# A one-dimensional average pool over 512 MB: larger input tiles, pairwise sums in place of a reduction, and another order of the last stores

## The chip, the cores and the metric

The kernel runs on one core of one Trainium2 chip. The metric is the time of one execution on the device in microseconds (us); the median of a few runs is quoted. The engines that matter here are VectorE (DVE in the profile), ScalarE (ACT), SyncE (SP), which only issues transfers here, and the 16 DMA engines of the core, which move data between HBM and SBUF, the on-chip memory of 128 partitions.

## The reference

The input `x` has 64 x 256 rows of 8192 float32. Each row is cut into windows of 4 elements that do not overlap, and the output is the mean of each window, 2048 values per row.

```
for i in range(out_len):                 # out_len = (8192 - 4) // 4 + 1 = 2048
    start = i * stride                   # stride = kernel_size = 4
    output[:, :, i] = np.mean(x[:, :, start : start + kernel_size], axis=2)
```

So 536.87 MB are read, 134.22 MB are written, and there are three additions and one scaling for each output.

## The kernel before

The shapes send the call to `_packed_fast_path` (the other path of the file, with its loops over `NT`, is not used). It takes F = 4 neighbouring rows for each partition, so that one group is 512 rows: 128 partitions with 32,768 consecutive input elements (128 KB) and 8192 consecutive output elements (32 KB) each. There are 32 groups, the loop over `t`.

In a group the loop over `f` handles the four rows one after the other. Each step takes a tile `xt` of 8192 elements (32 KB) per partition from the pool `xin`, which has three buffers. One load fills it from the SP queue (L245), one `tensor_reduce` on VectorE sums each window of four into a quarter of the output tile `ot` (L246), and `nc.scalar.mul` scales that quarter by 1/4 in place on ScalarE (L252). When all four quarters are there, one store of 32 KB per partition goes out from the ACT queue (L253). `ot` has two buffers.

A load can be issued as soon as its buffer is free, that is when the reduction three steps earlier has read it. The loads are issued in program order by SP, which waits for that reduction. The framework places all waits from these buffers; no order is written out by hand, except at the end.

The last group (from L258) is cut finer. Its row 0 is one load; rows 1 and 2 are each loaded in three pieces of about 2730 elements (L263, with reductions at L266 and scalings at L272). Row 3 is loaded in a ladder of six pieces that shrink from 2268 to 608 elements (L284, reductions at L293). Five of these pieces are scaled on ScalarE (L309) and stored from the ACT queue (L310); the last is scaled on VectorE into a small tile `fin` (L300) and stored from SP (L307). Rows 0 to 2 of this group, 24 KB per partition, are held back: they are stored from SP in four pieces right after the last load was issued (L292), so that the DMA engines have work while the last pieces are reduced.

```
if last:
    qw = hold // _N_PARK
    for qi in range(_N_PARK):
        ...
        nc.sync.dma_start(out=ov[:, qa:qb], in_=ot[:, qa:qb])
```

Of the kernel before, what the change touches and what calls it, by code (L numbers as in the profile page):

```python
# [7 lines left out]
_N_PARK = 4  # L8
_FINAL_COLS_TGT = 608
_LADDER_RATIO = 1.39  # L10
_NCHUNK_PRE = 3
_PACK_STORES = True
_PACK_F_MAX = 4


def _tail_ladder(total: int, k: int, final: int, ratio: float = _LADDER_RATIO,
                 max_chunks: int = 12) -> list:
    if total < 4 * final:
        return [total]
    rev = []  # L20
    s = 0
    w = float(final)
    while len(rev) < max_chunks - 1:
        wi = max(k, (int(round(w)) // k) * k)
        if s + wi > total - k:
            break
        rev.append(wi)
        s += wi
        w *= ratio
    sizes = [total - s] + rev[::-1]  # L30
    assert sum(sizes) == total and all(x > 0 and x % k == 0 for x in sizes)
    return sizes


def _even_chunks(total: int, k: int, n: int) -> list:
    n = max(1, min(n, total // k))
    q = (total // n) // k * k
    sizes = [q] * n
    sizes[-1] += total - q * n
    assert sum(sizes) == total and all(s > 0 and s % k == 0 for s in sizes)  # L40
    return sizes


@with_exitstack
def kernel(
    ctx: ExitStack,
    tc: tile.TileContext,
    x: bass.AP,
    kernel_size: bass.AP,
    stride: bass.AP,  # L50
    out: bass.AP,
):
    nc = tc.nc

    K = int(kernel_size)
    S = int(stride)
    assert K == S, "only stride == kernel_size supported"

    B, C, L = x.shape
    OL = (L - K) // S + 1  # L60
    assert OL * K <= L

    P = nc.NUM_PARTITIONS

    xf = x.flatten_outer_dims()
    of = out.flatten_outer_dims()
    rows = B * C

    inv_k = 1.0 / float(K)
    dt = x.dtype  # L70
    IL = OL * K

    if _PACK_STORES and IL == L:
        F = 0
        for cand in range(_PACK_F_MAX, 1, -1):
            if rows % (P * cand) == 0 and (rows // (P * cand)) >= 2:
                F = cand
                break
        if F >= 2 and L >= 64 * K and OL % 8 == 0 and OL * F * 4 <= 32768:
            _packed_fast_path(nc, tc, xf, of, rows, L, OL, K, F, inv_k, dt, P)  # L80
            return

    RPP = 1
    R = P * RPP
    NT = rows // R
    IL2 = RPP * L
    OL2 = RPP * OL
    fast = (
        IL == L
        and rows % R == 0  # L90
        and NT >= 6
        and IL2 >= 64 * K
        and OL % 2 == 0
    )

    if not fast:
        with (
            tc.tile_pool(name="xin", bufs=4) as pin,
            tc.tile_pool(name="res", bufs=4) as pout,
        ):  # L100
            r0 = 0
            while r0 < rows:
                rn = min(P, rows - r0)
                xt = pin.tile([P, IL], dt)
                ot = pout.tile([P, OL], dt)
                nc.sync.dma_start(out=xt[:rn], in_=xf[r0 : r0 + rn, :IL])
                nc.vector.tensor_reduce(
                    out=ot[:rn],
                    in_=xt[:rn].rearrange("p (m k) -> p m k", k=K),
                    axis=mybir.AxisListType.X,  # L110
                    op=mybir.AluOpType.add,
                )
                nc.scalar.mul(ot[:rn], ot[:rn], inv_k)
                nc.scalar.dma_start(out=of[r0 : r0 + rn], in_=ot[:rn])
                r0 += P
        return

    def xview(t):
        return xf[t * R : (t + 1) * R]

    def oview(t):
        return of[t * R : (t + 1) * R]

    ladder = _tail_ladder(IL2, K, _FINAL_COLS_TGT)
    chunks_pre = _even_chunks(IL2, K, _NCHUNK_PRE)
    fin_w = ladder[-1] // K

    with (
        tc.tile_pool(name="xin", bufs=4) as pin,
        tc.tile_pool(name="res", bufs=4) as pout,  # L130
        tc.tile_pool(name="rsv", bufs=1) as prsv,
        tc.tile_pool(name="fin", bufs=1) as pfin,
    ):
        rsv = prsv.tile([P, OL2], dt)
        fin = pfin.tile([P, fin_w], dt)

        for t in range(NT):
            xv = xview(t)
            ov = oview(t)
            xt = pin.tile([P, IL2], dt)  # L140
            ot = rsv if t == 0 else pout.tile([P, OL2], dt)

            if t == 0:
                nc.sync.dma_start(out=xt[:, :IL2], in_=xv[:, :IL2])
                nc.vector.tensor_reduce(
                    out=ot[:, :OL2],
                    in_=xt[:, :IL2].rearrange("p (m k) -> p m k", k=K),
                    axis=mybir.AxisListType.X,
                    op=mybir.AluOpType.add,
                )  # L150
                nc.scalar.mul(ot[:, :OL2], ot[:, :OL2], inv_k)
            elif t < NT - 3:
                nc.sync.dma_start(out=xt[:, :IL2], in_=xv[:, :IL2])
                nc.vector.tensor_reduce(
                    out=ot[:, :OL2],
                    in_=xt[:, :IL2].rearrange("p (m k) -> p m k", k=K),
                    axis=mybir.AxisListType.X,
                    op=mybir.AluOpType.add,
                )
                nc.scalar.mul(ot[:, :OL2], ot[:, :OL2], inv_k)  # L160
                nc.scalar.dma_start(out=ov[:, :OL2], in_=ot[:, :OL2])
            elif t < NT - 1:
                c0 = 0
                for cw in chunks_pre:
                    c1 = c0 + cw
                    o0, o1 = c0 // K, c1 // K
                    nc.sync.dma_start(out=xt[:, c0:c1], in_=xv[:, c0:c1])
                    nc.vector.tensor_reduce(
                        out=ot[:, o0:o1],
                        in_=xt[:, c0:c1].rearrange("p (m k) -> p m k", k=K),  # L170
                        axis=mybir.AxisListType.X,
                        op=mybir.AluOpType.add,
                    )
                    nc.scalar.mul(ot[:, o0:o1], ot[:, o0:o1], inv_k)
                    nc.scalar.dma_start(out=ov[:, o0:o1], in_=ot[:, o0:o1])
                    c0 = c1
            else:
                nchunk = len(ladder)
                c0 = 0
                for i, cw in enumerate(ladder):  # L180
                    c1 = c0 + cw
                    o0, o1 = c0 // K, c1 // K
                    last = i == nchunk - 1
                    nc.sync.dma_start(out=xt[:, c0:c1], in_=xv[:, c0:c1])
                    if last:
                        q0 = 0
                        qw = (OL2 - q0) // _N_PARK
                        for qi in range(_N_PARK):
                            qa = q0 + qi * qw
                            qb = q0 + (qi + 1) * qw if qi != _N_PARK - 1 else OL2  # L190
                            nc.sync.dma_start(
                                out=oview(0)[:, qa:qb], in_=rsv[:, qa:qb]
                            )
                    nc.vector.tensor_reduce(
                        out=ot[:, o0:o1],
                        in_=xt[:, c0:c1].rearrange("p (m k) -> p m k", k=K),
                        axis=mybir.AxisListType.X,
                        op=mybir.AluOpType.add,
                    )
                    if last:  # L200
                        nc.vector.tensor_scalar(
                            out=fin[:, :fin_w],
                            in0=ot[:, o0:o1],
                            scalar1=inv_k,
                            scalar2=None,
                            op0=mybir.AluOpType.mult,
                        )
                        nc.sync.dma_start(out=ov[:, o0:o1], in_=fin[:, :fin_w])
                    else:
                        nc.scalar.mul(ot[:, o0:o1], ot[:, o0:o1], inv_k)  # L210
                        nc.scalar.dma_start(out=ov[:, o0:o1], in_=ot[:, o0:o1])
                    c0 = c1


def _packed_fast_path(nc, tc, xf, of, rows, L, OL, K, F, inv_k, dt, P):
    R = P * F
    NTM = rows // R

# [10 lines left out]
    with (  # L229
# [6 lines left out]
        for t in range(NTM):  # L236
            xv = xe(t)
# [109 lines left out]
```

## Time and profile before

| | |
|---|---|
| median of 3 runs (lowest, highest) | 1561.05 us (1560.87, 1561.38) |
| span of the profiled execution, first to last instruction | 1559.0 us |
| VectorE busy | 1112.8 us (71%) in 138 instructions |
| ScalarE busy | 247.4 us (16%) |
| read from HBM, written to HBM | 536.87 MB, 134.22 MB |
| DMA rate over the span | 430 GB/s |

The profile gives of its execution the span, and no other time; the median of the runs is 2.0 us above that span, and these 2.0 us lie outside the first and the last instruction. The profile also has groups of instructions (line, engine, operation, output and input tile, count, busy time, mean duration, and the idle time before them with what ended it), a timeline in order of time, and windows, which tell for a stretch of time how long each engine was busy and what the DMA engines moved. "DMA share" is the mean busy share of the 16 DMA engines; as overlapping packets are both counted, it can be a little over 1.

### The profile page before, as it was taken

The numbers are of one execution on the slowest core, as the hardware profiler recorded it, in microseconds if no ns is written. First come the engines' busy times: TensorE is split into PE (matmuls) and PEld (weight loads), VectorE is DVE, ScalarE is ACT, GpSimd is POOL, SyncE is SP. The second block draws the span as 40 slices with busy tenths as digits, with TensorE's granted clock in tenths as the row PEclk, the third lists the DMA queues.
The fourth block names the chain that finished last, engine by engine and source line by source line (L and its number), as shares of the span: only waits on it lengthen the run. The fifth ranks groups of instructions, "written<-read, shape, count | busy, mean of one in ns | idle before, by whom it ended". The sixth has DMA issues, their size and how long they took to land.

```text
span 1559.0 us, 724 instructions
## 1 busy us (share of the span) xinstructions
DVE 1112.8 (71%) x138; ACT 247.4 (16%) x137; POOL 0.2 (0%) x4
## 2 busy tenths in 40 slices
DVE  6777667776667866677666776667766677766786
ACT  1111111111111111111111111111111111111111
POOL 0000000000000000000000000000000000000000
DMA  9999999999999999999999999999999999999999
GB/s 416 418 430 436 437 432 430 430 430 432 439 433 430 430 432 430 438 434 431 430 432 430 435 434 433 431 431 430 433 437 433 432 430 431 430 437 434 432 427 384
DMA packets 25637, 671.14 MB, mean 430 GB/s; under 512 B 2848, under 2 KB 3488, under 8 KB 4768
## 3 DMA queue, kind: packets, MB, share of 16 engines
q1 hardware_dynamic: 20448, 540.10, 80.6%
q10 hardware_dynamic: 5184, 131.00, 19.5%
q14 instruction: 5, 0.04, 0.0%
HBM read 536.87 MB, written 134.22 MB: 430 GB/s over the span
## 4 chain that ended last, share of the span: by engine, by line
DMA 75%; DVE 24%; issue 0%; SPq 0%; DVEq 0%
DMA xt<-in_x_dram 75%; DVE ot L246 23%; DVE ot L293 1%; DVE ot L266 0%; SPq L263 0%; DVEq L246 0%; DVE fin L300 0%
## 5 line engine op out<-in xcount | busy, mean ns | idle before, releaser
L246 DVE TENSOR_REDUCE ot<-xt 128x2048 f32<-128x8192 f32 x124 | 1077.1, 8686 | 430.2 <-DMA xt<-in_x_dram 430.2
L252 ACT ACTIVATE ot<-ot 128x2048 f32<-128x2048 f32 x124 | 237.0, 1911 | 1270.2 <-DVE ot L246 1270.2
L266 DVE TENSOR_REDUCE ot<-xt 128x682 f32<-128x2728 f32 (+2 forms) x7 | 26.6, 3809 | 6.9 <-DMA xt<-in_x_dram 6.9
L272 ACT ACTIVATE ot<-ot 128x682 f32<-128x682 f32 (+2 forms) x7 | 6.6, 936 | 25.8 <-DVE ot L266 25.8
L293 DVE TENSOR_REDUCE ot<-xt 128x417 f32<-128x1668 f32 (+5 forms) x6 | 9.0, 1568 | 0.0
L309 ACT ACTIVATE ot<-ot 128x417 f32<-128x417 f32 (+4 forms) x5 | 2.6, 521 | 5.2 <-DVE ot L293 5.2
L252 ACT ACT_TABLE_LOAD x1 | 1.3, 1283 | 0.7 <-PEq L328 0.7
L300 DVE TENSOR_SCALAR fin<-ot 128x152 f32<-128x152 f32 x1 | 0.2, 239 | 0.0
L328 POOL MEMSET const-bfloat16-1.0<- 128x1 bf16 x1 | 0.1, 102 | 0.0
L328 POOL MEMSET const-uint8-127<- 128x1 uint8 x1 | 0.1, 102 | 0.0
L328 POOL MEMSET const-float32-0.0<- 128x1 f32 x1 | 0.1, 99 | 0.2 <-issue 0.2
L328 POOL MEMSET const-float32-1.0<- 128x1 f32 x1 | 0.1, 99 | 0.0
## 6 DMA issues: line engine op xcount, KB each, us to landing
xt<-in_x_dram SPq DMA_DIRECT2D x125, 4096.0 KB, 26.4
out_dram<-ot ACTq DMA_DIRECT2D x31, 4096.0 KB, 23.2
xt<-in_x_dram SPq DMA_DIRECT2D x4, 1364.0 KB, 23.4
out_dram<-ot SPq DMA_DIRECT2D x4, 768.0 KB, 7.7
xt<-in_x_dram SPq DMA_DIRECT2D x2, 1368.0 KB, 29.5
xt<-in_x_dram SPq DMA_DIRECT2D x1, 1134.0 KB, 16.2
xt<-in_x_dram SPq DMA_DIRECT2D x1, 834.0 KB, 22.6
xt<-in_x_dram SPq DMA_DIRECT2D x1, 816.0 KB, 17.8
```

Source lines behind the costliest of these rows:

```text
L246: nc.vector.tensor_reduce(out=ot[:, o0 : o0 + OL], in_=xt[:, :L].rearrange("p (m k) -> p m k", k=K), axis=mybir.AxisListType.X, op=mybir.A ...
L252: nc.scalar.mul(ot[:, o0 : o0 + OL], ot[:, o0 : o0 + OL], inv_k)
L266: nc.vector.tensor_reduce(out=ot[:, o0:o1], in_=xt[:, c0:c1].rearrange("p (m k) -> p m k", k=K), axis=mybir.AxisListType.X, op=mybir.AluOp ...
L272: nc.scalar.mul(ot[:, o0:o1], ot[:, o0:o1], inv_k)
L293: nc.vector.tensor_reduce(out=ot[:, o0:o1], in_=xt[:, c0:c1].rearrange("p (m k) -> p m k", k=K), axis=mybir.AxisListType.X, op=mybir.AluOp ...
L300: nc.vector.tensor_scalar(out=fin[:, :fin_w], in0=ot[:, o0:o1], scalar1=inv_k, scalar2=None, op0=mybir.AluOpType.mult,)
L309: nc.scalar.mul(ot[:, o0:o1], ot[:, o0:o1], inv_k)
L328: nc = _bacc.Bacc("TRN2", target_bir_lowering=False, num_devices=1)
```

## The change

The whole kernel is written anew. The grouping of rows, 128 KB of input and 32 KB of output per partition and group, is the same, and so are the addresses and sizes of the loads and stores outside the last groups. What differs:

- A tile `xt` has 16,384 elements (64 KB) per partition, and the pool has two of them in place of three of 32 KB. Two loads of 32 KB per partition fill one tile (L71). A group has two tiles, 64 in all (the loop over `n`).
- The sum of four is taken in two steps by `tensor_tensor` on VectorE, over the whole tile: neighbours are added in place into the tile's first half (L52: 8192 outputs), then neighbours of these sums go to `ot` (L57: 4096 outputs). ScalarE scales 4096 elements at once (L58).
- A store from the ACT queue (L84) follows each group up to group 29. Those of groups 30 and 31 are issued from SP after the last load.
- The last tile is loaded in two pieces of 11,264 and 5,120 elements. Behind them SP issues the store of all of group 30 (L74) and of the first half of group 31 (L75), and then one store for each of the two pieces (L81) when it is summed and scaled. The three-piece rows, the ladder, `fin`, and the five small stores from ACT are gone.

```diff
-        tc.tile_pool(name="xin", bufs=3) as pin,
-        tc.tile_pool(name="res", bufs=2) as pout,
-        tc.tile_pool(name="fin", bufs=1) as pfin,
...
-                    xt = pin.tile([P, L], dt)
-                    o0 = f * OL
-                    nc.sync.dma_start(out=xt[:, :L], in_=xv[:, f * L : (f + 1) * L])
-                    nc.vector.tensor_reduce(
-                        out=ot[:, o0 : o0 + OL],
-                        in_=xt[:, :L].rearrange("p (m k) -> p m k", k=K),
-                        axis=mybir.AxisListType.X,
-                        op=mybir.AluOpType.add,
-                    )
-                    nc.scalar.mul(ot[:, o0 : o0 + OL], ot[:, o0 : o0 + OL], inv_k)
-                nc.scalar.dma_start(out=ov[:, : F * OL], in_=ot[:, : F * OL])
...
+LOAD = 16384
+PER_STORE = 2
+HALVES = (8192, 8192)
+LAST = (11264, 5120)
...
+    run = LOAD * PER_STORE
+    total = x.shape[0] * x.shape[1] * x.shape[2]
+    groups = total // (P * run)
...
+    pin = ctx.enter_context(tc.tile_pool(name="xin", bufs=2))
+    pout = ctx.enter_context(tc.tile_pool(name="res", bufs=2))
 
+    def pool(xt, at, width, ot, to):
+        half = width // 2
+        four = xt[:, at : at + width].rearrange("p (m k) -> p m k", k=2)
+        nc.vector.tensor_tensor(
+            out=xt[:, at : at + half], in0=four[:, :, 0], in1=four[:, :, 1], op=ADD
+        )
+        two = xt[:, at : at + half].rearrange("p (m k) -> p m k", k=2)
+        o = ot[:, to : to + width // K]
+        nc.vector.tensor_tensor(out=o, in0=two[:, :, 0], in1=two[:, :, 1], op=ADD)
+        nc.scalar.mul(o, o, inv_k)
...
+    for n in range(groups * PER_STORE):
+        g, j = divmod(n, PER_STORE)
+        last = n == groups * PER_STORE - 1
+        if j == 0:
+            tiles[g] = pout.tile([P, run // K], dt, name="ot")
+        ot = tiles[g]
+        xt = pin.tile([P, LOAD], dt)
+        at = 0
+        for w in LAST if last else HALVES:
+            lo = j * LOAD + at
+            nc.sync.dma_start(out=xt[:, at : at + w], in_=xg[g][:, lo : lo + w])
+            at += w
+        if last:
+            nc.sync.dma_start(out=og[g - 1], in_=tiles[g - 1][:, :])
+            nc.sync.dma_start(out=og[g][:, : j * LOAD // K], in_=ot[:, : j * LOAD // K])
+        at = 0
+        for w in LAST if last else (LOAD,):
+            to = (j * LOAD + at) // K
+            pool(xt, at, w, ot, to)
+            if last:
+                nc.sync.dma_start(out=og[g][:, to : to + w // K], in_=ot[:, to : to + w // K])
+            at += w
+        if j == PER_STORE - 1 and g < groups - 2:
+            nc.scalar.dma_start(out=og[g], in_=ot[:, :])
```

More of the change, by code (lines that the diff above doesn't have):

```diff
@@ L6 @@
 from concourse._compat import with_exitstack
[L8 to L41, printed above, removed]
+ADD = mybir.AluOpType.add
+LOAD = 16384
+PER_STORE = 2
+HALVES = (8192, 8192)
+LAST = (11264, 5120)
 @with_exitstack
@@ L55 @@
     K = int(kernel_size)
[L56 to L61, printed above, removed]
+    assert K == 4 and int(stride) == 4 and x.shape[-1] % 4 == 0
     P = nc.NUM_PARTITIONS
[L65 to L69, printed above, removed]
     dt = x.dtype
[L71 to L93, printed above, removed]
-    )
[L96 to L106, printed above, removed]
-                nc.vector.tensor_reduce(
-                    out=ot[:rn],
-                    in_=xt[:rn].rearrange("p (m k) -> p m k", k=K),
-                    axis=mybir.AxisListType.X,
-                    op=mybir.AluOpType.add,
-                )
[L113 to L131, printed above, removed]
-        tc.tile_pool(name="fin", bufs=1) as pfin,
[L133 to L212, printed above, removed]
@@ L215, in _packed_fast_path @@
-def _packed_fast_path(nc, tc, xf, of, rows, L, OL, K, F, inv_k, dt, P):
-    R = P * F
-    NTM = rows // R
-    ladder = _tail_ladder(L, K, _FINAL_COLS_TGT)
-    chunks_pre = _even_chunks(L, K, _NCHUNK_PRE)
-    fin_w = ladder[-1] // K
-    def xe(t):
-        return xf[t * R : (t + 1) * R].rearrange("(p f) m -> p (f m)", f=F)
-    def oe(t):
-        return of[t * R : (t + 1) * R].rearrange("(p f) m -> p (f m)", f=F)
-    with (
-        tc.tile_pool(name="xin", bufs=3) as pin,
-        tc.tile_pool(name="res", bufs=2) as pout,
-        tc.tile_pool(name="fin", bufs=1) as pfin,
-    ):
-        fin = pfin.tile([P, fin_w], dt)
-        for t in range(NTM):
-            xv = xe(t)
-            ov = oe(t)
-            ot = pout.tile([P, F * OL], dt)
-            if t < NTM - 1:
-                for f in range(F):
-                    xt = pin.tile([P, L], dt)
-                    o0 = f * OL
-                    nc.sync.dma_start(out=xt[:, :L], in_=xv[:, f * L : (f + 1) * L])
-                    nc.vector.tensor_reduce(
-                        out=ot[:, o0 : o0 + OL],
-                        in_=xt[:, :L].rearrange("p (m k) -> p m k", k=K),
-                        axis=mybir.AxisListType.X,
-                        op=mybir.AluOpType.add,
-                    )
-                    nc.scalar.mul(ot[:, o0 : o0 + OL], ot[:, o0 : o0 + OL], inv_k)
-                nc.scalar.dma_start(out=ov[:, : F * OL], in_=ot[:, : F * OL])
-                continue
-            for f in range(F - 1):
-                xt = pin.tile([P, L], dt)
-                widths = [L] if f < F - 3 else chunks_pre
-                c0 = 0
-                for cw in widths:
-                    c1 = c0 + cw
-                    o0, o1 = f * OL + c0 // K, f * OL + c1 // K
-                    nc.sync.dma_start(
-                        out=xt[:, c0:c1], in_=xv[:, f * L + c0 : f * L + c1]
-                    )
-                    nc.vector.tensor_reduce(
-                        out=ot[:, o0:o1],
-                        in_=xt[:, c0:c1].rearrange("p (m k) -> p m k", k=K),
-                        axis=mybir.AxisListType.X,
-                        op=mybir.AluOpType.add,
-                    )
-                    nc.scalar.mul(ot[:, o0:o1], ot[:, o0:o1], inv_k)
-                    c0 = c1
-            fq = F - 1
-            xt = pin.tile([P, L], dt)
-            hold = fq * OL
-            nchunk = len(ladder)
-            c0 = 0
-            for i, cw in enumerate(ladder):
-                c1 = c0 + cw
-                o0, o1 = fq * OL + c0 // K, fq * OL + c1 // K
-                last = i == nchunk - 1
-                nc.sync.dma_start(
-                    out=xt[:, c0:c1], in_=xv[:, fq * L + c0 : fq * L + c1]
-                )
-                if last:
-                    qw = hold // _N_PARK
-                    for qi in range(_N_PARK):
-                        qa = qi * qw
-                        qb = (qi + 1) * qw if qi != _N_PARK - 1 else hold
-                        nc.sync.dma_start(out=ov[:, qa:qb], in_=ot[:, qa:qb])
-                nc.vector.tensor_reduce(
-                    out=ot[:, o0:o1],
-                    in_=xt[:, c0:c1].rearrange("p (m k) -> p m k", k=K),
-                    axis=mybir.AxisListType.X,
-                    op=mybir.AluOpType.add,
-                )
-                if last:
-                    nc.vector.tensor_scalar(
-                        out=fin[:, :fin_w],
-                        in0=ot[:, o0:o1],
-                        scalar1=inv_k,
-                        scalar2=None,
-                        op0=mybir.AluOpType.mult,
-                    )
-                    nc.sync.dma_start(out=ov[:, o0:o1], in_=fin[:, :fin_w])
-                else:
-                    nc.scalar.mul(ot[:, o0:o1], ot[:, o0:o1], inv_k)
-                    nc.scalar.dma_start(out=ov[:, o0:o1], in_=ot[:, o0:o1])
-                c0 = c1
@@ new lines @@
+    inv_k = 1.0 / K
+    run = LOAD * PER_STORE
+    total = x.shape[0] * x.shape[1] * x.shape[2]
+    groups = total // (P * run)
+    assert groups * P * run == total and groups >= 2
+    xg = x.flatten_outer_dims().rearrange("r l -> (r l)").rearrange("(g p w) -> g p w", p=P, w=run)
+    og = out.flatten_outer_dims().rearrange("r l -> (r l)").rearrange(
+        "(g p w) -> g p w", p=P, w=run // K
+    )
+    pin = ctx.enter_context(tc.tile_pool(name="xin", bufs=2))
+    pout = ctx.enter_context(tc.tile_pool(name="res", bufs=2))
@@ new lines @@
+    tiles = {}
+    for n in range(groups * PER_STORE):
[22 more added lines that the diff above has]
+            nc.scalar.dma_start(out=og[g], in_=ot[:, :])
```

## The prediction

> **What bounds the kernel now.** I read the page first: busy times, the row of DMA rates, the two queues.
>
> ```profile
> span 1559.0 us, 724 instructions
> DVE 1112.8 (71%) x138; ACT 247.4 (16%) x137; POOL 0.2 (0%) x4
> ...
> DMA  9999999999999999999999999999999999999999
> ...
> q1 hardware_dynamic: 20448, 540.10, 80.6%
> q10 hardware_dynamic: 5184, 131.00, 19.5%
> ```
>
> The packets of the two queues (SP's q1, ACT's q10) fill 100% of the time of 16 DMA engines. The kernel is bound by transfers; VectorE waits 430 us for loads. Any time to gain is where the engines are not busy, or busy and moving little. The windows show where that is (columns: length; busy time of DVE, ACT, POOL; clock; DMA share; GB/s).
>
> ```profile
> 10.00:50.00 40.00, 34.21 (x4) 5.73 (x3) 0.00 (x0) 1.00 1.00 433
> 50.00:54.00 4.00, 2.97 (x2) 1.91 (x1) 0.00 (x0) 1.00 0.91 393
> 54.00:58.00 4.00, 4.00 (x1) 0.00 (x0) 0.00 (x0) 1.00 1.09 369
> 58.00:60.00 2.00, 2.00 (x1) 0.00 (x0) 0.00 (x0) 1.00 0.72 311
> ...
> 1500.00:1520.00 20.00, 18.86 (x3) 3.82 (x3) 0.00 (x0) 1.00 1.00 428
> 1520.00:1540.00 20.00, 14.26 (x5) 3.86 (x5) 0.00 (x0) 1.00 1.00 423
> 1540.00:1550.00 10.00, 9.91 (x8) 3.38 (x6) 0.00 (x0) 1.00 1.02 413
> ...
> 1552.00:1554.00 2.00, 0.00 (x0) 0.00 (x0) 0.00 (x0) 1.00 1.08 405
> 1554.00:1556.00 2.00, 0.00 (x0) 0.00 (x0) 0.00 (x0) 1.00 0.88 344
> 1556.00:1557.00 1.00, 0.00 (x0) 0.00 (x0) 0.00 (x0) 1.00 0.18 71
> ```
>
> From 60 to 1500 us every window of 200 us gives 432 or 433 GB/s: nothing is left there. Near 50 to 60 us, where ACT issues its first store (52.51 us), the rate dips; against 433 GB/s this loses 0.37 + 0.59 + 0.56 = 1.5 us. Later stores show no dip. From 1500 to 1554 the engines are fully busy but move less, in the stretch of small pieces; from 1554 some engines are done before others.
>
> Third, groups by form and the timeline, for durations.
>
> ```profile
> L246 DVE TENSOR_REDUCE ot<-xt 128x2048 f32<-128x8192 f32 x124 | 1077.1, 8686 | 430.2 <-DMA xt<-in_x_dram 430.2
> L252 ACT ACTIVATE ot<-ot 128x2048 f32<-128x2048 f32 x124 | 237.0, 1911 | 1270.2 <-DVE ot L246 1270.2
> L266 DVE TENSOR_REDUCE ot<-xt 128x682 f32<-128x2728 f32 x4 | 12.0, 2993 | 1.5 <-DMA xt<-in_x_dram 1.5
> L272 ACT ACTIVATE ot<-ot 128x682 f32<-128x682 f32 x4 | 3.1, 772 | 9.2 <-DVE ot L266 9.2
> L300 DVE TENSOR_SCALAR fin<-ot 128x152 f32<-128x152 f32 x1 | 0.2, 239 | 0.0
> ```
>
> The first load is issued at 0.73 us and the first reduction starts at 12.74; the next start at 22.43, 32.14 and 41.85. So a load of 4.19 MB takes 9.70 us of the engines (432 GB/s), and issue plus landing add 12.01 - 9.70 = 2.3 us.
>
> **The change, part by part.** *Loads and stores.* The bytes, addresses and 32 KB rows of 126 loads and 30 ACT stores are as before; at 432 GB/s they cost the same. The question is only whether the SP queue ever runs dry.
>
> *Sums.* VectorE goes from 8.69 us per 8192 inputs to two passes per 16,384. No row shows a tensor-tensor addition or an operand with a step of two. The two reduction rows give (8686 - 2993) / (8192 - 2728) = 1.042 ns per element and 151 ns fixed. If a pass costs by its outputs (two operands read side by side), it is 8.69 + 4.42 = 13.1 us per tile. If it costs by the inputs read, one at a time, it is 17.2 + 8.7 = 25.9 us. The low end is the L300 row's (239 - 151) / 152 = 0.58 ns per element: 7.4 us. I take 13.1, since the reduction's row is one element per step and an addition step makes one output. VectorE's sum is 64 x 13.1 = about 840 us (54%). ACT takes 4096 elements at 0.834 ns + 203 ns (its two rows) = 3.6 us, 232 us in all, hidden beside loads.
>
> *Two buffers.* A tile's two loads take 2 x 9.70 = 19.4 us of the engines. When tile n lands, tile n+1 is queued; tile n+2 is issued after the two passes and its data flows 2.3 us later (this counts landing too). The queue is refilled 13.1 + 2.3 = 15.4 us after the landing, 4.0 us before tile n+1 is through. A store in flight only lengthens that cover. So no gap, and both signs of the VectorE price up to 17.1 us per tile cost nothing. Before, the margin was 2 x 9.70 - 8.69 - 2.3 = 8.4 us.
>
> *Added waits.* Pass 1 waits for two loads in place of one; behind it are pass 2, the scaling and SP's next loads, all counted above. Pass 2 waits for pass 1: L300, which reads what L293 just wrote, starts at 1549.71, 0.04 us after L293's last end. Pass 2 of a new group also waits for the store two groups back, issued over 50 us earlier, where stores land within 23.2 us. At the end SP waits at L75 for the scaling of tile 62 and has only L81's stores behind it.
>
> The Trainium skill ("VectorE: DVE Perf Modes", section "The DRAIN you can't avoid") puts a drain of the operation's duration less 266 ns behind every VectorE operation. Taken as coming on top, it would start pass 2 8.4 us later, the tile would take 21.5 us, and by the rival's price below the time would be about 1700 us. The six back-to-back reductions at L293, 9.0 us busy in 9.02 us of the timeline, speak against that reading.
>
> *The tail.* Removed: six loads of 1364 to 1368 KB, six ladder loads, five small ACT stores, L307, four stores of 768 KB. What they cost is the fully busy stretch below 433 GB/s: 20 x 5/433 + 20 x 10/433 + 10 x 20/433 = 1.15 us up to 1550, and 0.08 (416 GB/s) + 0.13 from there to 1554: 1.4 us. Added: two load pieces, the half store, and two stores of 1408 and 640 KB. The first three have rows of 16 KB or more, larger than the cut rows were: taken as 0.1 us. The last two move 2.1 MB in 4.8 us at 2 to 5% loss: 0.15 us. Net -1.1 us; bounds 0 and -1.4.
>
> Does the last sum hide? From the last landing L, the queue still holds group 30 (4.19 MB, 9.7 us) and half of group 31 (4.85 us): busy until L + 14.5. Tile 62 landed at L - 19.4, and its passes end at about L - 5.7; piece one takes 5632 and 2816 outputs, 9.1 us, to L + 3.4; piece two 4.3 us, to L + 7.7; its scaling 1.3 us, and at most the 2.3 us of issue, to L + 11.3. That is 3.2 us before the parked stores are through, and piece one's store lies between (3.3 us). So the queue stays full to the last byte. What remains is the spread of the engines after 1554 and the end after the last landing: (2 - 1.59) + 0.84 + 0.97 + 1.04 = 3.3 us, kept.
>
> The Trainium skill ("DMA: Bandwidth & Descriptors", section "Anatomy of one DMA") gives each transfer about 2.0 us of fixed cost. There are 178 issues before and 162 after; if each cost were exposed, 16 x 2.0 = 32 us would go, to 1529 us. The landings 9.70 us apart while loads are queued say that it is hidden.
>
> **Sum.** Span 1559.0 - 1.1 = 1557.9 us; the 2.0 us outside it are kept: 1559.9 us.
>
> **The rivals.** 0.2% is 3.1 us, about what a measurement of this kernel can tell from no change.
>
> *Slower: VectorE starves the queue.* It decides from 17.1 us per tile on. Beyond that the engines stand idle once per group of two tiles (a store covers the other boundary), 32 us for each us. At the by-input price of 25.9 us, a tile's loads take 21.7 us after issue, 31.4 with a store in between; the pace alternates between 25.9 and 31.4, 28.7 x 64 = 1835 us. For it: no row shows such an addition, with two operands of step two and an output over its own input. Against it: 13.1 would have to be wrong by 30%. 0.12.
>
> *Slower, a little: two buffers do not keep the queue full*, because an engine that lags delays the landing, by more than the 4.0 us of margin. A gap of 0.1 us per tile is 6.4 us: 1566 us. The spread after 1554, some 2 to 3 us, speaks against it. 0.06.
>
> *Faster: more of the losses go.* If the dip at 50 to 60 us (-1.5) does not come back and the engines end 1 us closer together, it is 1557.4 us. For it: stores after the first show no dip; against it: ACT still has a first store. 0.13.
>
> *The forecast*, 0.69, has its own range of 1558.3 to 1561.5: 1559.9 and the tail's bounds, with the spread of the engines 1 us either way.
>
> **Numbers.** Faster by over 0.2% (below 1557.9) is the faster rival, 0.13; same 0.69; slower 0.12 + 0.06 = 0.18. The range goes down to 1556.5 (the tail's full 1.4, the dip's 1.5 and 1.6 of the spread) and up to 1566, the small gap's price; what is left out is mostly the starved queue.
>
> **What would show it.** Right: L52 near 8.7 and L57 near 4.4 us, VectorE near 54%; windows at 432 to 433 GB/s from 60 us to some 10 us before the end, also past 1540; a dip near 57 us. Wrong: windows below 430 in the middle, or passes of 17 us and more together (starved queue); a higher rate in the middle than 433 would break the argument altogether, since I hold that for what the engines can do.

## The result, and the profile after

The changed kernel takes 1569.18 us, the median of 5 runs (1567.99 to 1570.91), against 1561.15 us for the kernel before in the same comparison: a ratio of 1.0052, 95% interval 1.0040 to 1.0064. It is slower by 8.0 us, or 0.5%, where 1559.9 us and no measurable change were predicted; the range ended at 1566.0. Medians in this document are over all runs of a kernel; the ratios are not quotients of these medians and leave out one disturbed run of e8, so that the two can differ a little where the runs scatter (e8, e9, h4, k2).

The page of the changed kernel (its profiled execution took 1570.91 us):

```profile
span 1569.1 us, 619 instructions
DVE 839.8 (54%) x130; ACT 232.9 (15%) x66; POOL 0.2 (0%) x4
...
GB/s 414 414 439 430 429 433 433 429 434 433 431 430 430 433 427 425 430 426 434 423 434 433 430 429 427 424 425 422 433 433 429 428 431 433 427 423 433 427 435 379
...
q1 hardware_dynamic: 19008, 545.27, 81.4%
q10 hardware_dynamic: 4320, 125.83, 18.6%
```

The busy times are those of the prediction, and the two queues still fill 100% of the engines' time: nothing ran dry. But the row of rates, one number for each 39 us, falls below 430 again and again after the first third. The groups by form agree with the priced durations to 0.01 us:

```profile
L52 DVE TENSOR_TENSOR xt<-xt 128x8192 f32<-128x8192 f32 x63 | 547.6, 8693 | 712.1 <-DMA xt<-in_x_dram 712.1
L57 DVE TENSOR_TENSOR ot<-xt 128x4096 f32<-128x4096 f32 x63 | 278.8, 4425 | 3.8
L58 ACT ACTIVATE ot<-ot 128x4096 f32<-128x4096 f32 x63 | 227.8, 3616 | 1316.2 <-DVE ot L57 1316.2
```

The windows of the changed kernel (columns as in the prediction) show where the time is. The same windows of the kernel before give 433 GB/s; the second of them is shown below the others.

```profile
200.00:400.00 200.00, 106.77 (x17) 31.58 (x9) 0.00 (x0) 1.00 1.00 432
600.00:800.00 200.00, 109.31 (x17) 28.93 (x8) 0.00 (x0) 1.00 1.00 429
1000.00:1200.00 200.00, 109.04 (x17) 28.93 (x8) 0.00 (x0) 1.00 1.00 428
```

```profile
600.00:800.00 200.00, 143.87 (x17) 30.58 (x16) 0.00 (x0) 1.00 1.00 433
```

The DMA share is 1.00 in each of the four: after the change the engines are as busy, and move 1% less. 1% of the 1000 us from 500 to 1500 us is 10 us, the size of the loss. It is not in the tail.

To see what is slow I used the trace's record of each DMA packet, put in a row for each engine. A packet of 32 KB (one partition's row of a load or store) takes 1213 ns in both kernels, and the packets of an engine follow each other without gaps (0.3 us of idle time per engine in all). But some packets take longer. Summed over all 32-KB packets above 1230 ns, their time beyond 1213 ns, divided by 16 engines, is **before** 1.6 us up to 75 us (mainly at the first store) and 0.1 us from there on, from 5 packets; **after** 1.8 us and then 11.6 us, from 572 packets. This sum after 75 us is called the stretch below. The gap to a kernel without it, f1 below, is 11.1 us of span (1569.1 against 1558.0).

Some four fifths of this time is in load packets that run 0.5 to 4.5 us after an ACT store was issued, on each engine the one or two just before its first packet of that store. Around one store, the timeline of the changed kernel:

```profile
971.53 8.69 DVE L52 TENSOR_TENSOR xt<-xt 128x8192 f32<-128x8192 f32 x1 [16.75 <-DMA xt<-in_x_dram]
980.26 4.42 DVE L57 TENSOR_TENSOR ot<-xt 128x4096 f32<-128x4096 f32 x1
984.71 0.80 SPq L71 DMA_DIRECT2D xt<-in_x_dram  x2
984.71 3.62 ACT L58 ACTIVATE ot<-ot 128x4096 f32<-128x4096 f32 x1 [26.28 <-DVE ot L57]
988.36 0.34 ACTq L84 DMA_DIRECT2D out_dram<-ot  x1
990.96 8.69 DVE L52 TENSOR_TENSOR xt<-xt 128x8192 f32<-128x8192 f32 x1 [6.28 <-DMA xt<-in_x_dram]
```

and its windows from that store on, and between stores (a window counts each packet whole where it starts, so that short windows are exact only to some per cent):

```profile
988.00:1000.00 12.00, 8.95 (x2) 0.33 (x1) 0.00 (x0) 1.00 1.02 404
1006.00:1030.00 24.00, 9.02 (x2) 1.82 (x1) 0.00 (x0) 1.00 1.00 430
```

The tile that the queue is working on lands just before 990.96, when its pass 1 starts. The two loads behind it were issued at 984.71, the store at 988.36. So the engines cross from one tile's loads to the next one's right around the store's issue, and the 12 us from the store on run at 404 GB/s.

The loss builds up. By "spread" I mean the time between the first and the last of the 16 engines to finish the same load. In the kernel before it is 0.5 us early and 1.3 us at 850 us. In the changed kernel the stores up to 500 us cost 0.05 to 0.3 us each, on some of the engines; the spread grows from 0.4 to 3.4 us by 550 us. Of the 20 stores from 547.76 us on, 12 hit all 16 engines and cost 0.4 to 1.0 us each; the other 8 cost at most 0.3 us.

### The profile page after: what moved, and what is told of

Read it like the earlier page. It is cut to its first block, busy times and chain, and to the rows that moved or that the text cites. A ratio compares the mean times of both kernels' runs of the same rounds, so it can differ in the third digit from the quotient of the medians.

```text
span 1569.1 us, 619 instructions
## 1 busy us (share of the span) xinstructions
DVE 839.8 (54%) x130; ACT 232.9 (15%) x66; POOL 0.2 (0%) x4
## 4 chain that ended last, share of the span: by engine, by line
DMA 71%; DVE 27%; SPq 1%; issue 0%; ACT 0%; DVEq 0%
DMA xt<-in_x_dram 71%; DVE xt L52 18%; DVE ot L57 9%; SPq L71 1%; ACT ot L58 0%; DVEq L52 0%
## 5 line engine op out<-in xcount | busy, mean ns | idle before, releaser
L52 DVE TENSOR_TENSOR xt<-xt 128x8192 f32<-128x8192 f32 (+1 forms) x65 | 556.5, 8561 | 712.1 <-DMA xt<-in_x_dram 712.1
L58 ACT ACTIVATE ot<-ot 128x4096 f32<-128x4096 f32 (+1 forms) x65 | 231.6, 3564 | 1323.5 <-DVE ot L57 1323.5
L57 DVE TENSOR_TENSOR ot<-xt 128x4096 f32<-128x4096 f32 (+1 forms) x65 | 283.4, 4360 | 3.9
## 6 DMA issues: line engine op xcount, KB each, us to landing
out_dram<-ot SPq DMA_DIRECT2D x1, 1408.0 KB, 12.6
out_dram<-ot SPq DMA_DIRECT2D x1, 640.0 KB, 11.1
```

Of the source, the lines that this page charges most:

```text
L52: nc.vector.tensor_tensor(out=xt[:, at : at + half], in0=four[:, :, 0], in1=four[:, :, 1], op=ADD)
L57: nc.vector.tensor_tensor(out=o, in0=two[:, :, 0], in1=two[:, :, 1], op=ADD)
L58: nc.scalar.mul(o, o, inv_k)
```

## The experiments

The kernels are named by the labels e1 to k2. Unless it is said otherwise, diffs are against the changed kernel. Four theories were tested. *Store start*: an ACT store that starts while engines cross into freshly issued loads slows the loads. *Late refill*: with two buffers the next loads are issued only 1 to 6 us before an engine needs them, and that costs time by itself. *Burst*: two loads issued at once disturb the queue. *Sums*: the new VectorE passes disturb the DMA's writes into SBUF.

**e4, the sums alone** (the kernel before, its reduction replaced by the two passes).

```diff
-                    nc.vector.tensor_reduce(... ot[:, o0 : o0 + OL] ...)
+                    nc.vector.tensor_tensor(out=xt[:, : L // 2], in0=four[:, :, 0], in1=four[:, :, 1], ...)
+                    nc.vector.tensor_tensor(out=ot[:, o0 : o0 + OL], in0=two[:, :, 0], in1=two[:, :, 1], ...)
```

> The kernel before with the reduction at L246 replaced by the two pairwise passes, nothing else: three buffers of 32 KB, 6.7 us instead of 8.7 us per tile. Both theories: no change, 1560 to 1562 us; a store is issued 2 us earlier relative to the loads. If the pairwise passes themselves disturbed the transfers (two operands read, written in place): 1566 us or more.

1561.22 us (1560.91 to 1561.68), ratio 1.0001 (0.9993 to 1.0010). The pairwise sums by themselves change nothing in the time.

**e1, four tiles of 32 KB**, so that loads are queued deeper. Everything else, the tail too, is as changed.

```diff
-LOAD, PER_STORE, HALVES, LAST = 16384, 2, (8192, 8192), (11264, 5120)
+LOAD, PER_STORE, HALVES, LAST = 8192, 4, (8192,), (5632, 2560)
-    pin = ctx.enter_context(tc.tile_pool(name="xin", bufs=2))
+    pin = ctx.enter_context(tc.tile_pool(name="xin", bufs=4))
```

> The changed kernel with four buffers of 32 KB in place of two of 64 KB: one load, two passes and one scaling per 8192 elements, same SBUF, same stores, same tail order (last load in pieces of 5632 and 2560 elements). The queue is refilled some 20 us before it would run dry instead of 4. Store issue is about 9 us after a landing, again within 1 us of the next load boundary. Late-refill theory (engines that lead run out of queued loads): the loss goes, 1559 to 1561 us, rate 432 to 433 GB/s throughout. Store-start theory (a store that starts near a load boundary disturbs the engines whatever is queued): most of the loss stays, 1566 to 1570 us.

1560.27 us (1559.87 to 1560.76), ratio 0.9995 (0.9986 to 1.0004); stretch 0.2 us. The loss is gone, against the expectation from the store start. But the run also moves the store: the slowest engine crosses into the next load 0.5 us after the store's issue, where it is 2.1 us in the changed kernel. So it does not tell a deeper queue from a moved store.

**e3, no stores in the middle.** The ACT stores of groups 0 to 29 are left out.

```diff
-        if j == PER_STORE - 1 and g < groups - 2:
-            nc.scalar.dma_start(out=og[g], in_=ot[:, :])
```

> The changed kernel without the 30 stores from ACT (the outputs of groups 0 to 29 are not written). 125.8 MB less, 291 us at 432 GB/s. Every load boundary now has the short margin, not every second one. Late-refill theory: the loss stays or doubles, 1278 to 1290 us. Store-start theory: no loss, 1266 to 1269 us.

1270.37 us (1270.37 to 1270.54), ratio 0.8139 (0.8127 to 0.8150). Here every tile's loads are issued 3.3 to 5.4 us before the first engine needs them, and the stretch is 0.1 us. The time is 1.4 us above the upper end of what the store start gave, and 7.6 us below the lower end of the late refill. Late refill without stores costs nothing at this lead. (In the changed kernel the lead goes from 5.4 us down to 1.9 us as the spread grows, which e3 does not reach.)

**e2 and f1, the store later.** Each adds scalings by 1.0 on ScalarE before the ACT store (two in e2, one in f1), which delay it by 7.2 and 3.6 us and leave the loads alone.

```diff
+            half = ot[:, LOAD // 4 :]
+            nc.scalar.mul(half, half, 1.0)
             nc.scalar.dma_start(out=og[g], in_=ot[:, :])
```

> The changed kernel with two more scalings of the second half by 1.0 ahead of each store on ScalarE, so that the store is issued about 7.2 us later, some 6 us behind the load boundary instead of beside it. Loads, passes and the refill margin stay. Late-refill theory: 1567 to 1571 us, as the changed kernel. Store-start theory: 1559 to 1562 us.

> The changed kernel with one more scaling by 1.0 ahead of each store: the store is issued 3.6 us later, 7.3 us behind the loads, 1.5 to 3 us behind the load boundary, where the kernel before has its stores. Crossing: the loss is gone or nearly, 1559 to 1563 us; if it is the 4 to 8 us after the handing over of loads that count, wherever the boundary is: 1566 to 1571 us.

e2: 1559.98 us (1559.72 to 1562.28), ratio 0.9996 (0.9987 to 1.0005). f1: 1559.97 us (1559.66 to 1560.32), ratio 0.9993 (0.9984 to 1.0002). The stretch is 0.1 to 0.2 us in both. f1's windows, those of above and one from its store at 985.53 on:

```profile
200.00:400.00 200.00, 106.34 (x17) 48.01 (x14) 0.00 (x0) 1.00 1.00 433
600.00:800.00 200.00, 110.67 (x18) 43.40 (x12) 0.00 (x0) 1.00 1.00 433
1000.00:1200.00 200.00, 104.94 (x16) 44.74 (x13) 0.00 (x0) 1.00 1.00 433
...
985.00:997.00 12.00, 11.91 (x2) 0.51 (x1) 0.00 (x0) 1.00 0.99 429
```

ScalarE does more work, SP issues the next loads as long after a landing, and 9 us are gone.

**e5, the store earlier.** The second half of each group's outputs is not scaled (it is stored as sums), so the store goes out together with the next loads.

```diff
-        nc.scalar.mul(o, o, inv_k)
+        if scale:                      # j == 0 or last
+            nc.scalar.mul(o, o, inv_k)
```

> The changed kernel without the scaling of the second half of each group's output (it is stored as sums, not means), so that the store is issued right when pass 2 ends, together with the next tile's two loads and about 5.5 us ahead of the load boundary, instead of 3.6 us later. Theory burst (two loads and a store handed to the DMA queues within 4 us disturb the engines): the loss stays or grows, 1566 to 1572 us. Theory crossing (a store disturbs the engines when it starts while they cross into a load that was queued only some 5 us before): the store now starts before they cross, 1559 to 1563 us.

1559.89 us (1559.66 to 1560.37), ratio 0.9993 (0.9985 to 1.0002); stretch 0.1 us. Two loads and a store issued all at once cost nothing: the burst theory falls.

**e7, the burst with a deep queue**: e1 with each tile filled by two loads of 16 KB rows.

```diff
+LOAD, PER_STORE, HALVES, LAST = 8192, 4, (4096, 4096), (5632, 2560)     # bufs=4
```

> Four buffers of 32 KB as in the run with four tiles per group, but each tile filled by two loads of 16 KB per partition, issued together. Three other tiles are queued. The store is issued 2 us after two loads, at a load boundary. Burst: a loss of some us stays, 1564 to 1572 us. Crossing: none, since the load that the engines cross into was queued over 20 us before, 1559 to 1562 us.

1570.86 us (1570.70 to 1570.92), ratio 1.0063 (1.0051 to 1.0075). As slow as the changed kernel, for another reason: its rate is 429 to 431 GB/s in every window from 60 to 1500 us, and hardly any packets are stretched after 75 us (0.8 us in all). Its load packets of 16 KB take 614.6 ns on average where half of e1's 32-KB packet is 608.4; over 2032 such packets on each engine that is 12.6 us, against 10.6 us more span than e1. The run mixed two things and tells nothing of the burst; it shows what 16-KB rows cost.

**e8, one load of 64 KB rows for each tile.**

```diff
-HALVES = (8192, 8192)
+HALVES = (16384,)
```

> The changed kernel with one load of 64 KB per partition for each tile in place of two of 32 KB. Store and refill margin as in the changed kernel. Burst: one load and one store, as before the change: 1559 to 1562 us. Crossing: the loss stays, 1566 to 1572 us. (If 64 KB rows alone were slower, the windows away from the stores would fall below 432 GB/s.)

1569.23 us with a wide scatter (1561.32 to 1584.93), ratio 1.0062 (1.0033 to 1.0092). The profiled execution, the slowest of the ten, took 1584.93 us, with a stretch of 25.4 us in the 64-KB packets (2418 ns unstretched), again in the microseconds after store issues. A loss at the stores doesn't need two loads for a tile.

**e9 and f6, stores from SP.** e9 issues the group's store from SP where ACT issued it; SP thus waits for the scaling before it issues the next loads. f6 issues it from SP one group later, behind loads that are already out.

```diff
+        if j == 1 and 1 <= g < groups - 1:          # f6
+            nc.sync.dma_start(out=og[g - 1], in_=tiles[g - 1][:, :])
...
-            nc.scalar.dma_start(out=og[g], in_=ot[:, :])
+            nc.sync.dma_start(out=og[g], in_=ot[:, :])          # e9
```

> The changed kernel with the 30 stores issued from SP instead of ACT: they stand in the same queue as the loads, behind tile n+1 and ahead of tile n+2. Burst: two loads and a store are still handed over within some us, 1564 to 1572 us. Crossing, and any theory that needs two queues to interleave: no loss, 1558 to 1561 us.

> Stores from SP, each handed over behind the loads of the next tile but one, so that over 16 packets per engine are queued ahead of it and nothing is handed over late. Theory late handing over (the earlier SP run lost because each store was handed over 1 us before the queue ran dry): 1559 to 1562 us. Theory switch (an engine that goes from a store to a load in one queue loses 0.2 to 0.5 us each time): 30 x 0.3 us, 1566 to 1573 us.

e9: 1573.90 us (1572.59 to 1578.68), ratio 1.0093 (1.0078 to 1.0107), stretch 13.9 us. f6: 1562.35 us (1561.39 to 1562.83), ratio 1.0008 (0.9999 to 1.0016), stretch 2.3 us. e9 lies above both of its expected ranges, but it does not lose its time where the changed kernel does. 11.2 of its 13.9 us are in the last two store packets on each engine, 8 to 12 us after the store's issue, where the engines go over from the store to the load behind it. In f6, 2.0 of the 2.3 us are in the last two packets of the load ahead of the store. So with one queue and early issues most of the loss is gone, while with one queue and late issues another loss of the same size appears; whether the choice of queue matters for the loss at a store's start is not shown. The Trainium skill ("DMA: Bandwidth & Descriptors", section "Issuing engines are not separate DMA queues") says that DMAs from different engines end on the same 16 DMA engines and interleave, and that issuing from several saves the issuing time alone. The packet records agree: behind a store's first packet, load and store packets mostly alternate one by one on each engine.

**f3, the same store with loads issued 8.7 us earlier.** Pass 1 is left out (the output is not the mean), so buffers come free earlier; three extra scalings put the store back to nearly the same time after the landing.

```diff
-        nc.vector.tensor_tensor(
-            out=xt[:, at : at + half], in0=four[:, :, 0], in1=four[:, :, 1], op=ADD
-        )
...
+            for w in (4096, 4096, 1408):
+                part = ot[:, LOAD // 4 : LOAD // 4 + w]
+                nc.scalar.mul(part, part, 1.0)
```

> The changed kernel without pass 1 (pass 2 alone runs, on the tile's first half as it was loaded, so that the output is not the mean), and with three more scalings by 1.0 ahead of each store. The tile's two buffers, two loads of 32 KB and the time from landing to store issue (16.8 us) are those of the changed kernel; only the next loads are handed over 8.7 us earlier, 12 us instead of 3.7 us ahead of the store. Theory crossing (store start while the engines cross into a load that was handed over only some us before): 1559 to 1562 us. If a store start at a load boundary of a two-buffer kernel is enough: 1566 to 1571 us.

1562.93 us, scattered (1560.77 to 1565.00), ratio 1.0010 (1.0001 to 1.0019); stretch 0.8 us in the profiled execution of 1560.87 us. There the seven stores after the first still stretch some packets (0.5 us in all), and the spread goes to 3 us; then it stops. Earlier loads take away most of the loss, not all: this was one of f3's fastest executions, and its median is 3.0 us above that of f1.

**g1, an early transfer on the ACT queue.** A load of 512 bytes per partition from ACT at the start, on top of e1, asks whether the dip at the first store is the first use of a queue.

```diff
+    warm = ctx.enter_context(tc.tile_pool(name="warm", bufs=1)).tile([P, 128], dt, name="warm")
+    nc.scalar.dma_start(out=warm, in_=xg[0][:, :128])
```

> The four-buffer version with a small load of 512 bytes per partition issued from ACT at the very start. If the 1.0 to 1.5 us dip at the first store is the first use of the ACT queue, it goes: 1559.2 us and no dip near 52 us. If it belongs to the first store as such, 1560.3 us as without.

1560.42 us (1560.09 to 1560.77), ratio 0.9996 (0.9987 to 1.0005). The first store still stretches the loads by 1.0 us per engine: the dip belongs to the first store, not to the queue's first use.

**h1, h2, h3, h4, k1: the store moved in finer steps.** As f1, with 896 elements (h1), 2048 (h2), 4096 + 4096 + 2688 (h4) and three times 4096 (k1) scaled by 1.0; in h3 only half of the second scaling is done, and the rest is stored as sums.

```diff
+            for w in (896,):          # h2: (2048,); h4: (4096, 4096, 2688); k1: (4096, 4096, 4096)
+                part = ot[:, LOAD // 4 : LOAD // 4 + w]
+                nc.scalar.mul(part, part, 1.0)
             nc.scalar.dma_start(out=og[g], in_=ot[:, :])
```

> One extra scaling by 1.0 of 896 elements, about 0.95 us, delays each ACT store; the output is unchanged. The store then starts 1 us closer to the engines' crossing into the freshly handed-over load, from about 1 us before it to 1 to 2 us behind it. If the loss depends on where the store starts relative to that crossing, the store is still inside the harmful stretch: 1564 to 1570 us, with stretched load packets ahead of the stores. If any move of the store cures it, or the loss has to do with the two waits being equal by chance, about 1560 us.

> As the last, with 2048 elements, about 1.9 us: the store starts at the crossing or up to 1 us behind it. Between the changed kernel (1569) and the 3.6 us delay (1560). If the harmful stretch goes from 2 us before to 1 us behind the crossing, part of the loss stays: 1561 to 1566 us. If it ends at the crossing, 1560 us.

> Only the first half of each group's second scaling is done, which brings the ACT store forward by about 1.7 us (a quarter of the outputs of groups 0 to 29 stays a sum instead of a mean). The store starts some 3.7 us before the crossing. The stores 3.6 us earlier and 7.2 us later, which start 3 us and more before a crossing, lost nothing; if the stretch begins 2 to 3 us before the crossing, 1560 us. If it reaches further forward, 1562 to 1568 us.

> Three extra scalings by 1.0 (4096, 4096 and 2688 elements), about 9.7 us, delay each ACT store by the time of one load; the output is unchanged. The store then starts about 2 us before the engines cross from the first to the second load of the next tile, the same distance from a crossing as in the changed kernel, but the load crossed into was handed over some 15 us earlier. If a store at a crossing costs time whatever the load's lead, 1568 to 1570 us. If it takes a late load as well, 1560 to 1562 us.

> Three extra scalings by 1.0 of 4096 elements, about 10.9 us, delay each ACT store; the output is unchanged. Against the 9.5 us delay this is 1.2 us more, so the slowest engine should cross about 1 to 2 us after the store's issue in place of about 2 to 3. If the distance to the crossing decides, most of the loss goes: 1560 to 1565 us. If the loss of the 9.5 us delay came from a store in the middle of a tile, or from the busier ScalarE, it stays: 1571 to 1585 us.

Sorted by how far the store is moved. "Slowest crosses" is the time from a store's issue to the moment at which the last engine goes over to the next load (median over the stores from the fifteenth on; minus is before the issue; e1 and e4 are at +0.5; e2, h4 and k1 are counted to the crossing inside the next tile; in h4 and k1 every other store stands at the second value; above +4 the store's own packets already come in between). Stretch and spread (at 850 us) are those of the profiled execution; that of h4 was its fastest (1571.15 us).

| kernel | store moved by, us | slowest crosses, us | stretch, us | spread, us | median (range), us | ratio (95%) |
|---|---|---|---|---|---|---|
| e5 | -3.6 | +8.0 | 0.1 | 1.3 | 1559.89 (1559.66 to 1560.37) | 0.9993 (0.9985 to 1.0002) |
| h3 | -1.7 | +4.9 | 0.6 | 1.5 | 1560.93 (1559.99 to 1570.91) | 1.0009 (0.9995 to 1.0024) |
| changed | 0 | +2.1 | 11.6 | 3.0 | 1569.18 (1567.99 to 1570.91) | 1.0052 (1.0040 to 1.0064) |
| h1 | +1.0 | +1.1 | 0.3 | 1.7 | 1560.14 (1559.61 to 1566.22) | 0.9999 (0.9989 to 1.0008) |
| h2 | +1.9 | +0.1 | 0.1 | 1.7 | 1560.04 (1559.70 to 1560.28) | 0.9993 (0.9984 to 1.0003) |
| f1 | +3.6 | -1.6 | 0.1 | 1.5 | 1559.97 (1559.66 to 1560.32) | 0.9993 (0.9984 to 1.0002) |
| e2 | +7.2 | +5.7 | 0.2 | 1.4 | 1559.98 (1559.72 to 1562.28) | 0.9996 (0.9987 to 1.0005) |
| h4 | +9.7 | +2.0, +3.2 | 12.1 | 3.7 | 1584.71 (1571.15 to 1590.39) | 1.0139 (1.0090 to 1.0188) |
| k1 | +10.9 | +0.8, +3.2 | 0.6 | 1.3 | 1560.81 (1559.92 to 1564.68) | 1.0001 (0.9993 to 1.0010) |

The changed kernel and h1 over the same 600 us, the changed kernel first:

```profile
500.00:1100.00 600.00, 325.33 (x50) 86.78 (x24) 0.00 (x0) 1.00 1.00 428
```

```profile
500.00:1100.00 600.00, 327.42 (x50) 101.79 (x37) 0.00 (x0) 1.00 1.00 433
```

Three things follow. One microsecond is enough: with the store 1.0 us later, nine of h1's ten runs take 1559.6 to 1560.5 us. One run of h1 (1566.22) and two of h3 (1567.54 and 1570.91) took longer all the same; they were not profiled, so whether they lost at the stores is not shown. The distance is locked: the slowest engine's landing releases the passes, the scaling and the store, and that takes 0.5 us to the start of pass 1 and 988.36 - 971.53 = 16.8 us from there. So the store comes 19.4 - 17.3 = 2.1 us ahead of the same engine's next crossing, and the measured +2.1 is the same for the first stores and the last. So an engine that loses a little at a store does not drift out of the place where it loses. And a late load is not needed: in h4 the load crossed into was issued 11 to 18 us earlier, and its median is the highest of all. Windows of h4 and of k1, whose store comes 1.2 us later still:

```profile
500.00:1100.00 600.00, 326.84 (x50) 209.00 (x63) 0.00 (x0) 1.00 1.00 429
```

```profile
500.00:1100.00 600.00, 327.18 (x50) 225.66 (x63) 0.00 (x0) 1.00 1.00 433
```

In h4 the stores that cost most, 0.4 to 1.0 us from the store at 751.84 on, are mostly those at +2.0, as in the changed kernel; k1 has turned these into +0.8. But the distance alone is no law. Stores at +3.0 to +3.2 cost 0.1 to 0.3 us in h4's first third and nothing in k1; f3, at +2.1 throughout, loses little; k1's last three stores are at +2.1 and cost nothing; in the changed kernel 8 of the last 20 stores are nearly spared at +2.1; and h4's first stores at +2.0 cost nothing, while its engines are still close together. My expectation for k1 (1560 to 1565) came true, but its distance of 1 to 2 us was met only roughly, and only by every other store.

**k2, the 64 KB rows of e8 with f1's later store.**

```diff
-HALVES = (8192, 8192)
+HALVES = (16384,)
...
+            half = ot[:, LOAD // 4 :]
+            nc.scalar.mul(half, half, 1.0)
```

> One load of 64 KB per partition for each tile, and one extra scaling by 1.0 of 4096 elements before each ACT store (3.6 us); the output is unchanged. If the 64 KB rows lost their time at the store's start, as the 32 KB rows did, the loss is gone, and what is left is the packet: 2418 ns in place of two of 1213 ns, 0.33% of the 1248 us of loads, 4 us: 1555 to 1557 us. If the 64 KB rows are to blame in themselves, 1565 to 1580 us, as scattered as before.

1571.00 us (1564.48 to 1571.91), ratio 1.0048 (1.0032 to 1.0064), stretch 13.9 us, most of it in packets 1 to 7 us after store issues, spread 4.7 us. It is 11 us above f1, where the longer packets should have put it 4 us below. Its slowest engine crosses 0.3 us before the store's issue, a place at which h2 (+0.1) loses nothing with 32-KB rows. So the distance of +2.1 that e8 shares with the changed kernel does not explain e8's loss, or not alone.

**What is settled, and what stays open.** Shown: the loss is added up at the starts of the stores, at most 1 us at each; it lies in load packets that take longer, with no engine idle; moving nothing but the store's issue by 1 us removes it and by 9.7 us makes it worse; sums, burst and late refill by itself are not the cause. Every profiled execution that lost 9 us or more at its ACT stores (the changed kernel, e8, h4, k2) has a spread of 3 us and more at 850 us; f3 has the spread and hardly the loss, and e9, which loses as much in other packets, has a spread of 0.5 to 1.3 us. Open: what in the DMA engines stretches a load packet when a store is about to join; whether the spread is a cause or only a trace of the losses; why f3, at +2.1, keeps only about a third of the loss, why single stores at +2.1 are spared, and why the 64-KB rows are not at -0.3; and what the choice of queue does.

Of versions that compute everything, f1 at 1559.97 us, e2 at 1559.98 and h2 at 1560.04 are the fastest. They are 1.0 to 1.1 us below the kernel before in their own comparisons, which is less than the 0.2% that can be told from no change.

## Why the prediction was wrong

*Right: the prices.* Pass 1, pass 2 and the scaling (8.69, 4.43, 3.62 us) came as priced, VectorE at 839.8 us. Pass 2 starts 0.04 us after pass 1 ends (971.53 + 8.69 against 980.26), so the reading of the drain rule as an 8.4 us wait is refuted by the new operation itself. The rival in which VectorE starves the queue fell with these rows.

*Right: the tail, and the sum without the middle.* Forecast was a span of 1557.9 us. The profiled executions of f1, h2, e5, e2, h1 and k1, the changed kernel with its store moved, have spans of 1557.9 to 1558.2 us, and medians of 1559.9 to 1560.8. The tail's -1.1 us, the kept dip (1.4 to 1.7 us of stretch before 75 us in each of them) and the kept end hold to some tenths.

*Wrong: what a store costs.* The step that failed is in "Two buffers": "A store in flight only lengthens that cover. So no gap." There was no gap, as it says: the queue never ran dry. But the step, like "at 432 GB/s they cost the same" in "Loads and stores", treated the start of a store as free wherever it falls among the loads. That rested on the kernel before, where "Later stores show no dip"; its stores are issued 1.4 us and more after all engines crossed (-1.4 in the terms of the table). The change moved the store, in its queue order unchanged, to 2.1 us ahead of the slowest engine's crossing. This place could be seen beforehand: the landing-to-store time of 17.3 us, three priced durations and the hand-overs between them, stands against 19.4 us for the next tile. Its price could not; no row of the kernel before shows it. The missing term is 11.6 us.

*The rivals.* "Two buffers do not keep the queue full" had the place (between tiles), the sign and, at 1566 us, nearly the size, and 0.06. Its mechanism is not what happened: nothing was starved, and the loss needs no late loads. Its counterargument, a small spread in the kernel before, was no evidence for the changed kernel, where the spread is 3 us. "Faster: more of the losses go" lost on its own sign: the dip at the first store stays in every kernel with ACT stores, g1's included.

*The check named in advance worked.* "windows below 430 in the middle" was given as the sign of an error, and it is what the page shows. It was named as the sign of a starved queue, though, and the queue was not starved.

*Two slips without effect.* The forecast's own range of 1558.3 to 1561.5 does not follow from the parts it names: the tail's bounds of 0 and -1.4 us and 1 us either way for the spread give 1558.6 to 1562.0. And the 2.0 us of fixed cost for each transfer come from a section of the Trainium skill ("Anatomy of one DMA") on transfers issued from GpSimd, while all of these are issued from SP and ACT; what the runs show here is the 2.3 us of issue and landing of the first load. Neither number enters the sum.

## What to carry to other kernels

In a kernel that is bound by DMA, a transfer's cost can depend on when it is issued, though no engine is ever idle: compare each store's issue with the moments at which the queue goes from one load to the next, before and after a change, and if windows fall while the DMA share stays at 1.00, move the store by a microsecond or a few and measure. A computation that is "hidden" still sets that moment, because it sits between a landing and the next issue; a store issued 1 us later was worth 9 us here. Do not split rows below 32 KB without need (e7: 10.6 us), and don't expect longer rows to pay by their packet time alone (e8, k2).

## What the hardware showed that I had not expected

- A load packet takes 614.6 ns on average for 16 KB, 1213 ns for 32 KB and 2418 ns for 64 KB per partition (the last two unstretched): 26.7, 27.0 and 27.1 GB/s on each engine. The 16-KB rows made e7 10.6 us slower than e1.
- The first store of an execution stretches load packets by 0.8 to 1.1 us per engine in all these kernels with 32-KB loads and ACT stores, at each of the places tried, and also if the ACT queue was used before (g1: 1.0 us).
- One microsecond of delay on an engine that is busy 15% of the time changed a kernel's time by 9 us (h1), and a kernel with the same instructions in other amounts scattered over 19 us (h4).
